# A decoder trunk's MLPs: where two plain blocks stand among the half products, and when one set of combinations is formed

## The chip, the cores and the metric

The kernel runs on one core of one Trainium2 chip. The metric is the device time of one execution in microseconds (us); several runs are taken and their median is compared. TensorE (PE) multiplies matrices, VectorE (DVE) and ScalarE (ACT) work on elements, GpSimd (POOL) and SyncE (SP) here mostly issue DMAs. PSUM is the small memory that PE writes to, in banks of 128 x 512 floats; everything else lies in SBUF.

## The reference

Two layers, 256 tokens, model width 2048, float32. Layer 0 mixes with gated linear attention, layer 1 with sliding-window attention; after each comes the MLP on which this case turns:

```
def sqrelu_mlp(h, w1, w2):
    u = jax.nn.relu(h @ w1)
    return (u * u) @ w2
# x += mixer(rmsnorm(x)); x += sqrelu_mlp(rmsnorm(x)); w1: 2048 x 8192, w2: 8192 x 2048
```

## The kernel before

**Numbers in two halves.** Every float32 product is made of three matmuls: a weight block `w` is split into `wh` (a rounded copy, a cast on ACT at L115) and `wl = w - wh` (a subtraction on DVE at L116), the activations likewise, and PE sums high x high, high x low and low x high. `halve` does a 512 x 512 block in two halves of 128 x 1024 each: two casts and two subtractions for a block. It has four `wh` tiles of half a block each (`WHL`), so a cast waits until PE has done with the half block four halves back; three `wl` tiles (`WS`) and three `ws` tiles, into which SP loads a block of 1 MB. The tiles of a pool are handed out in turn, so a load waits for the block three loads back.

**Seven products in the place of eight.** In most of the MLP, a pair of 512 x 512 output blocks is computed by Strassen's scheme (in Winograd's form) for two of the four row blocks of the weights, with the tokens cut into two halves: seven *half products* (12 matmuls of 128 x 512 each) of sums of weights and sums of activations take the place of eight, and two more row blocks come in as four *plain blocks* (24 matmuls each). A half product needs weights that are themselves sums. They are made in place: `wx` is loaded, then a DMA with addition (issued by POOL: L245 in W1, L1098 in W2) adds the next block to it once the earlier use is over; `wy` is added to a loaded block on DVE (L303, L1179), and a loaded block is added to `wx` on DVE (L321, L1194). A plain block costs ACT and DVE as much as a half product, and PE twice as much.

**Order of the work.** The MLP runs in four quarters of the 8192 hidden columns. In a quarter there are two pairs of columns of W1 (`two_columns`, with the class `Seven`), then two pairs of output columns of W2 (`seven`). In the first quarter the first pair is computed with `gemm_wide` instead, without sums; the combinations of the MLP's input that the half products of W1 need are formed there (`form_sums`, due `KEEP` ticks after the start; a tick comes twice for each plain or wide block, once for a half product), and written to DRAM to be fetched again in the later quarters. In W1 a string of steps sets the order: a digit n is half product `p`n, two digits "ij" are the plain block of row block i and column j, and "e" takes the sums E and F. The code of `seven` writes the order of W2 out: A0, plain 21, E2, plain 31, D4, C6, plain 20, plain 30, D5, A1, C3 (the letter is the bank, the number the operand). Below, half products of W2 are named that way, and those of W1 by their step.

**What orders the engines.** The Tile framework lays out each engine's instructions ahead of time, by priority and by its own estimate of when operands are there; casts, subtractions, loads and weight additions have a raised priority (`WPRI`). On the chip every engine then takes its instructions strictly in that order, and an instruction that waits holds up all behind it on its engine.

Of the kernel before, what the change touches and what calls it, by code (L numbers as in the profile page):

```python
# [21 lines left out]
C = 512  # L22
# [19 lines left out]
MX = 2  # L42
COMB = (1, 3)
ORDERS = "1 21 3 7 31 e 5 20 30 6 2 4", "21 1 31 3 7 e 5 20 30 6 2 4"
KEEP = 9, 11
SQ = (3, 2)
ATT = (5, 3), (9, 6), (10, 8), (11, 10)

# [2 lines left out]
def yoco_kernel(ctx: ExitStack, tc: tile.TileContext, x, norms, mlp_w1, mlp_w2, a_w_in, w_glr, w_gate, a_g_o, a_w_o,  # L51
# [12 lines left out]
    def bank(shape, tag, dtype=F32):  # L64
        return ps[tag].tile(shape, dtype, name=tag, tag=tag)
# [7 lines left out]
    def later(n, fn):  # L73
        due.setdefault(now[0] + n, []).append(fn)

    def tick():
        now[0] += 1
        for fn in due.pop(now[0], ()):
            fn()

    def mm(o, l, r, start=True, stop=True, **kw):
        nc.tensor.matmul(o, lhsT=l, rhs=r, start=start, stop=stop, **kw)  # L82
# [23 lines left out]
    def halve(ws, o=C, n=2):  # L106

        whs = [wp.tile([P, 2, C], F32R, name="wh", tag="wh", bufs=WHL) for _ in range(2)]
        wl = wp.tile([P, 4, C], F32R, name="wl", tag="wl", bufs=WS)
        with tc.high_priority(offset=WPRI):  # L110
            for k in range(0, 4, n):
                wh = whs[k // 2]
                js, ks = slice(k % 2, k % 2 + n), slice(k, k + n)
                w = ws[k // 2] if isinstance(ws, list) else ws[:, ks, :o]
                nc.scalar.copy(out=wh[:, js, :o], in_=w)  # L115
                nc.vector.tensor_sub(out=wl[:, ks, :o], in0=w, in1=wh.bitcast(F32)[:, js, :o])  # L116
        return [(whs[k // 2][:, k % 2], wl[:, k]) for k in range(4)]

    def split_w(parts, step=4):
        ws = wp.tile([P, 4, C], F32, name="ws", tag="ws", bufs=WS)  # L120
        with tc.high_priority(offset=WPRI):
            for k in range(0, 4, step):
                ks = slice(k, k + step)
                o = 0
                for ap in parts:
                    n = ap.shape[1]
                    nc.sync.dma_start(out=ws[:, ks, o:o + n],
                                      in_=ap[k * P:(k + step) * P].rearrange("(k p) n -> p k n", p=P))
                    o += n
        return halve(ws, o, min(step, 2))  # L130
# [85 lines left out]
    class Seven:  # L216
# [63 lines left out]

        def run(self, after, order="1 21 3 7 31 e 5 20 30 6 2 4"):

            for step in order.split():
                if len(step) == 2:
                    i, j = int(step[0]), int(step[1])
                    self.plain(i, j, *("EF" if j else "AC"))
                else:
                    (self.ef if step == "e" else getattr(self, "p" + step))(after)
# [28 lines left out]
        def p2(self, after):  # L317
            b21 = self.load(1, 0)
            with tc.high_priority(offset=WPRI):
                for n in range(2):  # L320
                    nc.vector.tensor_add(out=self.wx[n], in0=self.wx[n], in1=b21[:, 2 * n:2 * n + 2])  # L321
            self.product("A", self.token(1, 0), b21)
            after["a"](self.banks["A"])

        def p4(self, after):
            after["c"](self.product("C", self.token(1, 1), self.wx))
# [614 lines left out]
    def mlp(w1, w2, act, r, gains):  # L941
# [19 lines left out]
        def form_sums(pairs, es, b):  # L961

            combine_act(es, act, b, room)
            if b:
                for a, o in zip(pairs, kept):
                    nc.sync.dma_start(out=o, in_=a.bitcast(F32))
# [7 lines left out]
        def two_columns(col, es, hs, put):  # L974


            x = mp.tile([P, 4, C], F32, name="wx", tag="wx")
            add = lambda o, i, j: nc.vector.tensor_add(out=o, in0=i, in1=j)  # L978
            sub = lambda o, i, j: nc.vector.tensor_sub(out=o, in0=i, in1=j)  # L979
            h, ef = {}, []  # L980

            def relu(o, i, t):
                nc.scalar.activation(out=o, in_=i, func=AF.Relu, scale=r[:, t:t + 1])

            def turn(j, t, h):
                tp = bank([P, 4, P], "tp")
                for k in range(4):
                    nc.tensor.transpose(out=tp[:, k, :], in_=h[:, k * P:(k + 1) * P], identity=ident)  # L988
                put(j, slice(t * P, (t + 1) * P), tp)

            def p1(p):
                h["v"], h["22"] = hs()
                nc.scalar.mul(out=h["v"], in_=p, mul=-1.0)

            def p5(p):
                h["21"], h["12"] = hs()
                nc.scalar.copy(out=h["21"], in_=p)

            def p56(p):
                v, x21, x12, x22 = (h[i] for i in ("v", "21", "12", "22"))  # L1000
                add(v, p, v)
                add(x12, ef[0], v)
                relu(x12, x12, 0)
                later(1, lambda: turn(1, 0, x12))
                sub(x22, v, x22)
                add(x22, ef[1], x22)
                relu(x22, x22, 1)
                later(2, lambda: turn(1, 1, x22))
                sub(x21, x21, v)

            def p2(p):
                relu(h["v"], p, 0)
                later(1, lambda: turn(0, 0, h["v"]))

            def p4(p):
                add(h["21"], p, h["21"])
                relu(h["21"], h["21"], 1)
                later(1, lambda: turn(0, 1, h["21"]))

            z = Seven(lambda i, j: w1[i * C:(i + 1) * C, col[j]:col[j] + C], act, es,  # L1020
                      [x[:, 2 * i:2 * i + 2] for i in range(2)],
                      lambda: mp.tile([P, 4, C], F32, name="wy", tag="wy", bufs=1))
            z.run({"p1": p1, "p7": lambda p: nc.scalar.copy(out=h["22"], in_=p),
                   "ef": lambda e, f: ef.extend((e, f)), "p5": p5, "p56": p56, "a": p2, "c": p4}, ORDERS[1])

        def h_ops():
            n = iter(range(2))
# [16 lines left out]
        def pause(n):  # L1044

            pt = small()
            for i in range(n):
                mm(pt[:, i:i + 1], ident, ones[:, 0:1])
# [31 lines left out]
        def seven(w, n, op, us, g, acts, gains, sq, nr):  # L1080
# [6 lines left out]
            def block(i, j):  # L1087
                return w[i * C:(i + 1) * C, (c0 + j) * C:(c0 + j + 1) * C]
# [13 lines left out]
            def use(b):  # L1102
                if b in banks:
                    return banks[b], False
                banks[b] = bank([P, C], "ms" if b in "EF" else "acc")
                return banks[b], True

            def product(b, o, ws):
                p, st = use(b)
                halves = halve(ws)  # L1110
                for k in range(4):
                    wh, wl = halves[k]
                    mm(p, op[o][:, 0, k], wh, st and k == 0, False, skip_group_check=True)
                    mm(p, op[o][:, 0, k], wl, False, False, skip_group_check=True)
                    mm(p, op[o][:, 1, k], wh, False, k == 3, skip_group_check=True)
                tick()
                return p

            def plain(i, j, b0, b1, apart=False):

                halves = split_w([block(i, j)])
                ah, al, _ = us[i]
                ps_ = [use(b) for b in (b0, b1)]
                order = [(k, t) for k in range(4) for t in range(NT)]
                for n, (k, t) in enumerate(sorted(order, key=lambda kt: kt[1]) if apart else order):
                    wh, wl = halves[k]
                    p, st = ps_[t]
                    tt = slice(t * P, (t + 1) * P)
                    mm(p, ah[:, k, tt], wh, st and k == 0, False, skip_group_check=True)
                    mm(p, ah[:, k, tt], wl, False, False, skip_group_check=True)  # L1130
                    mm(p, al[:, k, tt], wh, False, k == 3, skip_group_check=True)
                    if n % 4 == 3:
                        tick()
# [47 lines left out]
            more(x, 1, 1)  # L1181
            add(x21, p)
            sub(x22, product("C", 6, y))
            for i in (2, 3):
                plain(i, 0, "A", "C", i == 2)
            add(v, product("D", 5, x))
            if g == 3:
                add(x12, v)
# [4 lines left out]
            with tc.high_priority(offset=WPRI):  # L1193
                nc.vector.tensor_add(out=x, in0=x, in1=b21)  # L1194
            product("A", 1, b21)
            add(x11, banks["A"])
            if g == n + 2 == 3 and not gains:

# [20 lines left out]
        for g in range(4):  # L1219
# [15 lines left out]
            else:  # L1235
                for b in range(2):
                    later(KEEP[b], lambda b=b, sums=sums, es=es: form_sums(sums, es, b))
                later(RS + 3, lambda: pause(2))
# [32 lines left out]
            for n in range(2):  # L1271
                seven(w, n, op, us, g, acts, gains, sq, nr)
# [241 lines left out]
```

## Time and profile before

| | |
|---|---|
| median of 3 runs | 2027.87 us (2027.11 to 2028.26) |
| the profiled execution | 2028.39 us, of which the span of its instructions is 2026.7 us |
| granted TensorE clock | 1.00 |
| busy | PE 2007.9 us (99%), DVE 1694.3 (84%), ACT 1307.3 (65%), POOL 236.7 (12%) |
| HBM | 461.23 MB read, 6.29 MB written |

A page's shares say which engine is busy, not which one waits: PE's matmuls overlap in the record (one of 128 x 512 is listed with 390 ns, while the next one starts 227 ns after it), so that PE looks busy also where its matmuls start late. The distance between starts shows it.

### The profile page before, as it was taken

What the parts mean: (1) busy time and instruction counts of PE and PEld (TensorE: products, weight loads), DVE (VectorE), ACT (ScalarE), POOL (GpSimd) and SP (SyncE); (2) the same over time, 40 slices, a digit from 0 to 9 for tenths busy, and PEclk for the clock granted to TensorE, in tenths of its full rate; (3) what the DMA queues carried; (4) which work ended last, traced back from release to release, by engine and by line L of the source; (5) the groups of instructions that cost most, each with busy time, mean ns of one, the idle gap of its engine ahead of it and who ended that gap; (6) DMA issues with size and microseconds to landing.
All of it is one profiled execution on the core that took longest, in us unless ns stands there. A gap on an engine that the chain in (4) does not pass through costs nothing.

```text
span 2026.7 us, 25842 instructions
## 1 busy us (share of the span) xinstructions
PE 2007.9 (99%) x9714; PEld 1660.9 (82%) x9714; DVE 1694.3 (84%) x1878; ACT 1307.3 (65%) x1724; POOL 236.7 (12%) x243
## 2 busy tenths in 40 slices
PE   9999999999999999999999999999999999999999
PEld 8998888887888788888788878788788888888887
DVE  6698787888888988987999676878988988988887
ACT  6746666666557657756767677656657756755765
POOL 2251110000010010001101121000010001101000
PEclk9999999999999999999999999999999999999999
DMA  8445775778898799888876543788799898889875
GB/s 287 146 156 177 216 220 188 204 248 253 264 294 251 229 297 263 231 281 267 237 225 193 166 137 122 206 261 248 225 301 262 231 282 272 237 259 294 256 228 147
DMA packets 237037, 469.21 MB, mean 232 GB/s; under 512 B 8704, under 2 KB 19216, under 8 KB 234864
## 3 DMA queue, kind: packets, MB, share of 16 engines
q1 hardware_dynamic: 195296, 380.92, 54.0%
q0 software_dynamic: 38528, 84.76, 22.5%
q10 hardware_dynamic: 3088, 1.88, 0.3%
q8 instruction: 76, 1.25, 0.2%
q14 instruction: 49, 0.40, 0.1%
HBM read 461.23 MB, written 6.29 MB: 231 GB/s over the span
## 4 chain that ended last, share of the span: by engine, by line
PE 70%; issue 10%; DVE 9%; DMA 8%; ACT 3%; POOL 1%; ACTq 0%; POOLq 0%; DVEq 0%
PE acc L82 51%; PE ms L82 14%; DMA wx<-in_mlp_w_dram 7%; DVE wl L116 5%; PE tp L82 3%; ACT sc L1397 1%; ACT wh L115 1%; DVE h L978 1%; PE tp L988 1%; DMA ws<-in_a_w_in_dram 1%; POOL wx L245 1%; PE tp L833 0%; DVE h L979 0%; DVE sc L1407 0%; DVE wx L321 0%
## 5 line engine op out<-in xcount | busy, mean ns | idle before, releaser
L82 PE MATMUL acc<-wh,act 128*128 128x512 f32 x2928 | 931.0, 392 | 1.2 <-ACT act L341 0.5
L115 ACT CAST wh<-ws 128x1024 fp32r<-128x1024 f32 x544 | 569.9, 1051 | 314.1 <-PE acc L82 235.4
L116 DVE TENSOR_TENSOR wl<-ws,wh 128x1024 fp32r<-128x1024 f32 x544 | 669.3, 1241 | 103.8 <-ACT wh L115 98.7
L82 PEld LDWEIGHTS acc<-wh,act 128*128 128x128 f32 x2928 | 548.3, 188 | 119.1 <-ACT wh L115 2.2
L82 PE MATMUL acc<-wl,act 128*128 128x512 f32 x1464 | 571.4, 390 | 1.2 <-DVE wl L116 1.2
L116 DVE TENSOR_TENSOR wl<-wx,wh 128x1024 fp32r<-128x1024 f32 x272 | 328.3, 1222 | 108.9 <-ACT wh L115 104.5
L115 ACT CAST wh<-wx 128x1024 fp32r<-128x1024 f32 x272 | 285.6, 1053 | 204.5 <-PE acc L82 100.9
L82 PEld LDWEIGHTS acc<-wl,act 128*128 128x128 f32 x1464 | 275.0, 188 | 58.0 <-DVE wl L116 2.1
L82 PE MATMUL ms<-wh,act 128*128 128x512 f32 x512 | 166.7, 393 | 2.1 <-DVE act L1268 2.1
L82 PE MATMUL acc<-act,wh 128*128 128x256 f32 (+1 forms) x640 | 141.4, 308 | 0.9 <-ACT wh L403 0.9
L115 ACT CAST wh<-wy 128x1024 fp32r<-128x1024 f32 x92 | 96.1, 1054 | 62.3 <-PE ms L82 49.9
L116 DVE TENSOR_TENSOR wl<-wy,wh 128x1024 fp32r<-128x1024 f32 x92 | 111.1, 1222 | 20.8 <-ACT wh L115 19.0
L82 PE MATMUL acc<-wh,ops 128*128 128x512 f32 (+1 forms) x392 | 124.8, 390 | 0.6 <-DVE h L978 0.6
L245 POOL DMA_DIRECT2D wx<-in_mlp_w_dram x56 | 67.9, 1237 | 485.1 <-DVE wl L116 424.1
L82 PE MATMUL acc<-wh,op 128*128 128x512 f32 x384 | 123.4, 389 | 0.0
L82 PEld LDWEIGHTS ms<-wh,act 128*128 128x128 f32 x512 | 95.5, 188 | 25.6 <-DVE act L1268 5.5
L1098 POOL DMA_DIRECT2D wx<-in_mlp_w_dram x32 | 41.2, 1287 | 597.4 <-DVE wl L116 583.0
L82 PEld LDWEIGHTS acc<-act,wh 128*128 128x128 f32 x640 | 104.5, 191 | 6.6 <-ACT wh L403 1.1
L82 PE MATMUL acc<-act,wl 128*128 128x256 f32 x384 | 107.9, 283 | 0.6 <-DVE wl L404 0.6
L82 PE MATMUL ms<-wl,act 128*128 128x512 f32 x256 | 99.8, 390 | 0.0
L82 PE MATMUL tp<-wh,cmb 128*128 128x512 f32 x288 | 94.5, 389 | 0.0
L82 PEld LDWEIGHTS acc<-wh,ops 128*128 128x128 f32 x392 | 72.6, 188 | 15.3 <-ACT wh L115 1.6
(298 smaller groups left out, 2571.6 us busy)
## 6 DMA issues: line engine op xcount, KB each, us to landing
ws<-in_mlp_w_dram SPq DMA_DIRECT2D x196, 1024.0 KB, 7.0
ws<-in_a_w_in_dram SPq DMA_DIRECT2D x42, 1024.0 KB, 5.1
wx<-in_mlp_w_dram POOLq DMA_DIRECT2D x32, 1024.0 KB, 9.1
wy<-in_mlp_w_dram SPq DMA_DIRECT2D x30, 1024.0 KB, 7.4
wx<-in_mlp_w_dram POOLq DMA_DIRECT2D x56, 512.0 KB, 8.6
wx<-in_mlp_w_dram SPq DMA_DIRECT2D x16, 1024.0 KB, 5.0
ws<-in_b_w_q_dram SPq DMA_DIRECT2D x16, 1024.0 KB, 5.1
ws<-in_a_w_o_dram SPq DMA_DIRECT2D x15, 1024.0 KB, 5.2
```

Source lines behind the costliest of these rows:

```text
L82: nc.tensor.matmul(o, lhsT=l, rhs=r, start=start, stop=stop, **kw)
L115: nc.scalar.copy(out=wh[:, js, :o], in_=w)
L116: nc.vector.tensor_sub(out=wl[:, ks, :o], in0=w, in1=wh.bitcast(F32)[:, js, :o])
L245: nc.gpsimd.dma_start(out=o, in_=a, accum_op=ALU.add)
L978: add = lambda o, i, j: nc.vector.tensor_add(out=o, in0=i, in1=j)
L988: nc.tensor.transpose(out=tp[:, k, :], in_=h[:, k * P:(k + 1) * P], identity=ident)
L1098: nc.gpsimd.dma_start(out=ws, in_=block(i, j).rearrange("(k p) n -> p k n", p=P), accum_op=ALU.add)
L1397: nc.scalar.activation(out=sc[:, h], in_=sc[:, h], func=AF.Exp, bias=nmx[:, h:h + 1], scale=f[:, h:h + 1], accum_out=su[:, h:h + 1])
```

## The change

1. In W1 (`two_columns`) the order "21 1 31 3 7 e 5 20 30 6 2 4" becomes "1 21 3 31 5 7 20 e 6 2 30 a 4". The new step "a" hands bank A on after plain block 30 and not after `p2`, since 30 still adds to A.
2. In W2 (`seven`) plain block 30 moves from its place behind plain 20 to a place behind A1: D4, C6, plain 20, D5, A1, plain 30, C3.
3. `KEEP` goes from 9, 11 to 5, 7: the combinations of the MLP's input are formed four ticks sooner in the first quarter.

No matmul, cast, addition or byte is added or taken away.

```
-KEEP = 9, 11
+KEEP = 5, 7
...
         def run(self, after, order="1 21 3 7 31 e 5 20 30 6 2 4"):
+            self.late = "a" in order
             for step in order.split():
-                if len(step) == 2:
+                if step == "a":
+                    after["a"](self.banks["A"])
+                elif len(step) == 2:
...
             self.product("A", self.token(1, 0), b21)
-            after["a"](self.banks["A"])
+            if not self.late:
+                after["a"](self.banks["A"])
...
-                   "ef": lambda e, f: ef.extend((e, f)), "p5": p5, "p56": p56, "a": p2, "c": p4}, ORDERS[1])
+                   "ef": lambda e, f: ef.extend((e, f)), "p5": p5, "p56": p56, "a": p2, "c": p4}, "1 21 3 31 5 7 20 e 6 2 30 a 4")
...
-            for i in (2, 3):
-                plain(i, 0, "A", "C", i == 2)
+            plain(2, 0, "A", "C", True)
             add(v, product("D", 5, x))
...
             product("A", 1, b21)
+            plain(3, 0, "A", "C")
             add(x11, banks["A"])
```

The first place to see in the layout is DVE in W2, around D5 and A1, in the second pair of the third quarter. `wx` holds D5's weights, the block under L1194 (now L1197) is b21, A1's weight block; the `wl` behind it are A1's. Before:

```order
L116 TENSOR_TENSOR wl_7576<-ws_7572,wh_7574 128x1024
L1136 TENSOR_TENSOR xs_3309<-xs_3309,acc_7518 128x512
L116 TENSOR_TENSOR wl_7576<-ws_7572,wh_7575 128x1024
L116 TENSOR_TENSOR wl_7607<-wx_7378,wh_7605 128x1024
L116 TENSOR_TENSOR wl_7607<-wx_7378,wh_7606 128x1024
L1194 TENSOR_TENSOR wx_7378<-wx_7378,ws_7625 128x2048
L116 TENSOR_TENSOR wl_7630<-ws_7625,wh_7628 128x1024
L116 TENSOR_TENSOR wl_7630<-ws_7625,wh_7629 128x1024
```

And now:

```order
L116 TENSOR_TENSOR wl_7543<-ws_7539,wh_7542 128x1024
L116 TENSOR_TENSOR wl_7574<-wx_7378,wh_7572 128x1024
L1140 TENSOR_TENSOR xs_3309<-xs_3309,acc_7518 128x512
L116 TENSOR_TENSOR wl_7574<-wx_7378,wh_7573 128x1024
L1197 TENSOR_TENSOR wx_7378<-wx_7378,ws_7592 128x2048
L116 TENSOR_TENSOR wl_7597<-ws_7592,wh_7595 128x1024
L116 TENSOR_TENSOR wl_7597<-ws_7592,wh_7596 128x1024
L116 TENSOR_TENSOR wl_7618<-ws_7614,wh_7616 128x1024
```

D5's two subtractions, the addition and A1's two now come directly behind plain 20 (wl_7543), and those of plain 30 (wl_7576 before, wl_7618 now) behind them.

The second place is DVE a little later, where W2 ends and the next quarter's W1 begins. ws under L303 (now L306) is b12, the block to which `wy` is added for p7. Before, with C3's halves (wl_7650), plain 21's (wl_7684), p1's (wl_7720) and plain 31's (wl_7745):

```order
L116 TENSOR_TENSOR wl_7650<-wx_7378,wh_7649 128x1024
L116 TENSOR_TENSOR wl_7684<-ws_7680,wh_7682 128x1024
L1135 TENSOR_TENSOR xs_3267<-acc_7380,xs_3267 128x512
L116 TENSOR_TENSOR wl_7684<-ws_7680,wh_7683 128x1024
L116 TENSOR_TENSOR wl_7720<-wx_7679,wh_7718 128x1024
L116 TENSOR_TENSOR wl_7720<-wx_7679,wh_7719 128x1024
L1135 TENSOR_TENSOR xs_3267<-acc_7518,xs_3267 128x512
L303 TENSOR_TENSOR ws_7795<-ws_7795,wy_7774 128x2048
L116 TENSOR_TENSOR wl_7745<-ws_7741,wh_7743 128x1024
```

And now, with the second half of plain 30 (wl_7618), C3 (wl_7650), p1 (wl_7685) and plain 21 (wl_7710):

```order
L116 TENSOR_TENSOR wl_7618<-ws_7614,wh_7617 128x1024
L116 TENSOR_TENSOR wl_7650<-wx_7378,wh_7648 128x1024
L116 TENSOR_TENSOR wl_7650<-wx_7378,wh_7649 128x1024
L116 TENSOR_TENSOR wl_7685<-wx_7679,wh_7683 128x1024
L1139 TENSOR_TENSOR xs_3267<-acc_7380,xs_3267 128x512
L306 TENSOR_TENSOR ws_7819<-ws_7819,wy_7741 128x2048
L116 TENSOR_TENSOR wl_7685<-wx_7679,wh_7684 128x1024
L116 TENSOR_TENSOR wl_7710<-ws_7706,wh_7708 128x1024
```

The addition to b12 now stands in the middle of p1's subtractions, ahead of plain 21's, with four instructions between it and the subtraction that frees the tile b12 is loaded into: that of plain 30 (wl_7618). Before, b12's tile was that of A1's block, and nine instructions stood between. The layout is alike at the start of W1 in each quarter but the first.

## The prediction

> **What bounds the kernel now.** I read the page's busy times first, then the matmuls' spacing in the timeline and the chain of waits, then who waits for PE and for whom PE waits, and last the DMA queues.
>
> ```profile
> span 2026.7 us, 25842 instructions
> PE 2007.9 (99%) x9714; PEld 1660.9 (82%) x9714; DVE 1694.3 (84%) x1878; ACT 1307.3 (65%) x1724; POOL 236.7 (12%) x243
> 855.16 27.20 PE acc L82 x120
> 850.00:900.00 50.00, 50.00 (x222) 41.42 (x221) 43.26 (x42) 28.26 (x27) 3.85 (x3) 1.00 0.88 264
> 950.00:1000.00 50.00, 49.65 (x224) 40.09 (x223) 45.89 (x48) 36.82 (x45) 4.86 (x4) 1.00 0.79 234
> ```
>
> The third row is a piece of the chain of waits: 120 matmuls in 27.20 us, 0.2267 us apart, is PE's own pace; long stretches of the MLP run at it. The last two rows are 50 us of the third and fourth quarter: DVE works 43 to 46 of the 50 us, and the DMA engines are 0.79 to 0.88 busy. So PE sets the time, the change takes no matmul away, and it can win only what PE now loses by starting late. Those losses stand in few places:
>
> ```profile
> 467.64 0.39 PE L82 MATMUL acc<-wh,cmb 128*128 128x512 f32 x1
> 468.90 0.50 PE L82 MATMUL acc<-wl,cmb 128*128 128x512 f32 x1 [0.87 <-DVE wl L116]
> 490.94 0.39 PE L82 MATMUL acc<-wh,act 128*128 128x512 f32 x1
> 491.80 0.50 PE L82 MATMUL acc<-wl,act 128*128 128x512 f32 x1 [0.47 <-DVE wl L116]
> 960.90 0.39 PE L82 MATMUL acc<-wh,act 128*128 128x512 f32 x1
> 961.49 0.47 PE L82 MATMUL acc<-wh,act 128*128 128x512 f32 x1 [0.20 <-DVE h L978]
> 1009.56 0.40 PE L82 MATMUL ms<-wl,act 128*128 128x512 f32 x1
> 1010.15 0.73 PE L82 MATMUL ms<-wh,act 128*128 128x512 f32 x2 [0.20 <-DVE act L1268]
> PE ms L82 <- DVE act L1268: 2.1, 8, 0.3
> ```
>
> Starts 1.26, 0.86, 0.59 and 0.59 us apart where 0.23 would do: (i) p3 of the first quarter, late by 1.03; (ii) the end of W1 in the first quarter; (iii) the step from W1's first pair to its second; (iv) the step from W1 to W2, where plain 21 waits for activations that only the last half products give (the last row: in each of the eight quarters). Everywhere else in the MLP the matmuls keep their pace, which means that `wh` and `wl` are there in time, not that they are early.
>
> **The change, part by part.** *What it can win.* Adding up the same spacings over 0.2267 in each place: (iii) 0.3 to 1.1 us in six quarters, mean 0.6, so 3.8; (iv) 0.7 to 1.6, mean 0.8, so 4.9 in six quarters, of which I take 4, since p6's results now come 36 matmuls (8.2 us) ahead of W1's end and not 24; (ii) 2.3 in each layer's first quarter, of which I take 1.75, 3.5; (i) 1.5 with its neighbours in each layer, of which I take 1, so 2, because the two combination stores now stand ahead of three loads on SP. If forming the combinations sooner delays the first quarter's own operands, it costs as much as it gives: (i) from -3 to +3. Sum of the gains 13.3 (0 to 18).
>
> *W2: D5 and A1 come sooner, their operand doesn't.* In 16 places D5 now starts 48 matmuls after D4, 10.88 us, where it was 72, 16.32. D5's weights are `wx` plus a block that POOL may only add once DVE is done with D4:
>
> ```profile
> 893.47 1.28 POOL L1098 DMA_DIRECT2D wx<-in_mlp_w_dram  x1 [12.05 <-DVE wl L116]
> 895.80 0.39 PE L82 MATMUL acc<-wh,op 128*128 128x512 f32 x1
> 853.28 1.28 POOL L1098 DMA_DIRECT2D wx<-in_mlp_w_dram  x1 [15.39 <-DVE wl L116]
> 855.00 0.39 PE L82 MATMUL acc<-wh,op 128*128 128x512 f32 x1
> DMA to landing us min/median/max: 8.4/9.1/12.7
> wx<-in_mlp_w_dram POOLq DMA_DIRECT2D x1, 1024.0 KB, 11.4
> wx<-in_mlp_w_dram POOLq DMA_DIRECT2D x1, 1024.0 KB, 10.9
> ```
>
> The issue is 2.3 us ahead of D4's first matmul in the second pair (2.2 over its eight places) and 1.7 in the first. The fifth row is the source line of all 32 such DMAs; the last two are the first and last of the second pairs' eight, whose mean is 10.1 us (the first pairs' eight: 9.2). So the sum lands 7.9 us after D4's start in the second pair and 7.4 in the first. What DVE then has to do in its order is read from the order shown with the change and from these rows:
>
> ```profile
> 900.19 2.35 DVE L116 TENSOR_TENSOR wl<-ws,wh 128x1024 fp32r<-128x1024 f32 x2
> 902.46 0.68 DVE L1136 TENSOR_TENSOR xs<-xs,acc 128x512 f32<-128x512 f32 x1
> 903.06 1.22 DVE L116 TENSOR_TENSOR wl<-ws,wh 128x1024 fp32r<-128x1024 f32 x1
> 909.23 2.29 DVE L1194 TENSOR_TENSOR wx<-wx,ws 128x2048 f32<-128x2048 f32 x1
> 911.44 1.22 DVE L116 TENSOR_TENSOR wl<-ws,wh 128x1024 fp32r<-128x1024 f32 x1
> L115 ACT CAST wh<-wx 128x1024 fp32r<-128x1024 f32 x272 | 285.6, 1053 | 204.5 <-PE acc L82 100.9
> ```
>
> Start to start a subtraction takes 1.13 us, a 512-wide addition 0.60, the addition of b21 2.21; the last row is the cast, 1.05. From the landing: cast 1.15 with its waits, subtraction 1.13, addition to xs 0.60, subtraction 1.13, b21 2.21, A1's first subtraction 1.22: 7.45 us. A1 begins 60 matmuls after D4 and needs that half at its second matmul, at 13.6 + 0.23 = 13.83. So A1 is late by whatever the landing exceeds 6.4 us after D4's start. Second pairs: 7.9 - 6.4 = 1.5 each, 12 in eight. First pairs: 7.4 - 6.4 = 1.0; but the waits of (iv) go, and with them two additions of L1268 (0.69 each) from DVE's work ahead of D4, so that the issue comes about 0.7 sooner: 0.3 each, 2 in eight. Together 14 us; bounds 2, if all land in the 8.4 us of the quickest with that 0.7, and 27, if the second pairs take 12 us and the first keep their 1.0. Before, the same DMA had 5.4 us more, and PE never waited here.
>
> *W1: the addition for p7 stands in p1's way.* In six places (the first pair of W1 in the later quarters) DVE reaches b12's addition (L303) with only the loads' own time behind it. SP can load b12 once plain 30's second subtraction is done. From the landing of D5's weights that is: 7.45 - 1.22 to the start of A1's first subtraction, then 1.13, 1.13, 1.13 and 0.60 to that of plain 30's second half, and its 1.22: 11.4. The load has its rows before, the quickest and slowest of these six:
>
> ```profile
> ws<-in_mlp_w_dram SPq DMA_DIRECT2D x1, 1024.0 KB, 5.8
> ws<-in_mlp_w_dram SPq DMA_DIRECT2D x1, 1024.0 KB, 8.1
> 923.43 2.28 DVE L303 TENSOR_TENSOR ws<-ws,wy 128x2048 f32<-128x2048 f32 x1
> DVE wl L116 <- ACT wh L115: 222.2, 233, 4.6
> ```
>
> Mean 7.2. Then the addition, 2.2, and p1's second subtraction, 1.22: at 22.1. PE needs that half in p1's eighth matmul: A1 starts at 7.2 on the same clock, A1, plain 30 and C3 are 48 matmuls, 10.9, and 1.6 more: 19.7. Late by 2.4 each, 1.0 to 3.3 with the two rows: 14 us in six (6 to 20). DVE's long waits now are for ACT's casts (last row), short ones for loads. The second pair has the same addition in the same place, but there DVE has five more additions ahead of it and reaches it when the block is just there: 0 to 0.5 each. Behind the addition wait plain 21's and p3's subtractions on DVE; plain 21 gives them 5.4 us of PE for 2.3 of DVE, so nothing else is late.
>
> *p5 to p6.* 48 matmuls from p5's start to p6's, not 60 (10.9 us, not 13.6), and `wx` must be summed again between:
>
> ```profile
> 938.05 1.20 POOL L245 DMA_DIRECT2D wx<-in_mlp_w_dram  x1 [12.94 <-DVE wl L116]
> 939.42 1.20 POOL L245 DMA_DIRECT2D wx<-in_mlp_w_dram  x1 [0.17 <-issue]
> 939.32 0.39 PE L82 MATMUL tp<-wh,cmb 128*128 128x512 f32 x1
> ACT wh L115 <- DMA wx<-in_mlp_w_dram: 67.9, 30, 4.2
> DMA to landing us min/median/max: 5.9/8.4/12.0
> ```
>
> ACT waits here already (67.9 us in 30 waits). The second issue came 0.1 us after p5's start; with the median 8.4, a cast and a subtraction the half is there at 10.9, and p6 needs it at 10.9 + 1.6 = 12.5. p5 now stands behind a plain block, which gives its casts 2.7 us more lead: I take 0 to 1 us in all 14 pairs together, 1; with landings of 12 it is 2 each, 28.
>
> By the Trainium skill, "DMA: Bandwidth & Descriptors", section "Anatomy of one DMA — SWDGE (gpsimd) path", a DMA of POOL's kind takes about 2.0 us plus its bytes over 436e3 per us, an estimate of 4.4 us for the 1 MB of D5. By that A1 would never be late and the W2 term were 0. The 32 rows here, 8.4 us at the least, don't agree; it is the first rival's price in W2, no more.
>
> *Sum.* 14 + 14 + 1 + 1 - 13.3 = +16.7, with 1 for b12's addition in the second pairs; I take +16. The profiled execution is 2028.4 us, 0.5 above the median of the runs and inside their range: 2044.
>
> **The rivals.** *Only the gains* (faster): D5's sum and b12 land sooner than before, because the new order spreads the loads, and PE keeps its pace; 2028.4 - 13 = 2015. For it: DVE's and PE's work is unchanged, and losses (i) to (iv) are real. Against: none of the 32 additions landed in under 8.4 us, at DMA shares of 0.8 to 0.9. Chance 0.15. *Gains and losses cancel*: landings at their short ends, W2 2 to 4 and b12 6, against 10 to 13 gained; 2028. It needs both at once. 0.15. *p6 decides* (slower still): the second addition into `wx` lands after 10 us or more, so that each of 14 p6 is late by 1 to 2; it begins to cost at 10.0 us after p5's start, and adds some 21 to the forecast, 2065. For it: ACT's 30 waits; against it: the longer lead of p5. 0.12. The forecast itself 0.58.
>
> **How the numbers follow.** The likeliest is 2044, its own range 2032 to 2056 from the bounds of the two large terms, which will not all be met at one end. To hold 8 in 10 the range takes in "cancel" and stops short of most of the other two: 2022 to 2060. A difference of 0.2% (4 us) is what runs of this kernel tell from none. Faster: the first rival and a little of the second, 0.15. Same: the rest of the second and the forecast's low end, 0.15. Slower: 0.70.
>
> **What would show it.** W2: DVE's idle time ahead of D5's subtractions ended by a late cast, ACT's cast of `wx` ended by the DMA of line 1098's kind in all 16 places, and A1's second matmul 0.5 to 2 us late. W1: DVE idle ahead of the addition to b12, ended by the load of `ws`, and p1's eighth matmul late by 1 to 3 us in six places, not in the second pairs. (iii) and (iv) gone. If DVE doesn't wait at b12's addition, or A1 keeps PE's pace, the terms fall and the first rival is right; if p6 stands out, the third.

## The result and the profile after

The changed kernel takes 2086.4 us (median of four runs, 2083.1 to 2087.7), the kernel before 2027.5 beside it: 1.029 times as long (95% interval 1.027 to 1.031). The forecast was slower, 2044 us, with 2060 as the upper end of its range: the direction was right, the loss 3.7 times as large as forecast (59 us, not 16). The profiled execution of the changed kernel took 2083.1 us. The head of its page, which answers the first two rows shown of before:

```profile
span 2081.4 us, 25838 instructions
PE 2020.6 (97%) x9714; PEld 1668.6 (80%) x9714; DVE 1700.1 (82%) x1878; ACT 1311.9 (63%) x1724; POOL 238.2 (11%) x243
```

The span is 54.7 us longer and DVE has no more work than before (1700 us, 1694 before). PE's 2020.6 says little, since waiting matmuls are listed as busy in part; the list of waits says more. Of the changed kernel, for whom an engine waited, with the sum in us, the number of waits and the longest:

```profile
PE acc L82 <- DVE wl L116: 21.5, 6, 4.7
PE acc L82 <- DVE xs L1140: 16.1, 16, 2.9
PE acc L82 <- ACT h L1027: 12.1, 11, 2.7
DVE ws L306 <- DMA ws<-in_mlp_w_dram: 22.0, 6, 5.3
```

The first and the last belong together: six waits of PE behind b12's addition, as forecast but longer. The second and third are new, and neither waits for weights. L1140 in its 16 places takes C6 from `xs`, L1027 copies p7: both only *read a PSUM bank*, and PE waits because it wants to write there next.

Added up over the matmuls of each step, distance from start to start less PE's own pace (0.2267 us for 128x512, 0.07 allowed for a transpose), over 14 pairs of W1 and 15 of W2 (the last pair of W2 has another form):

| us over the pace | before | after |
|---|---|---|
| p1 of W1 | 0.5 | 27.7 |
| plain 20 of W1 | 0.0 | 15.8 |
| plain 20 of W2 | 0.4 | 21.7 |
| plain 30 and p4 of W1 | 1.8 | 7.6 |
| plain 21 of W1 | 8.2 | 7.4 |
| A0, plain 21, E2 of W2 | 14.9 | 4.2 |
| p3 and p2 of W1 | 5.2 | 0.0 |
| D5 and A1 of W2 | 0.0 | 0.1 |
| all steps | 30.7 | 85.1 |

The difference, 54.4 us, is nearly all of the longer span. Each transpose comes some 0.04 us later than the 0.07 allowed, so that the rows with transposes (plain 21, 30 and p4 of W1, A0 to E2 of W2) hold some of these too, and not only waits. D5 and A1, where the forecast put its first 14 us, lose nothing.

**Plain 20 of W2.** The timeline of the place that the prediction's order shows (third quarter, second pair; POOL, ACT, DVE, then PE):

```profile
910.75 1.28 POOL L1102 DMA_DIRECT2D wx<-in_mlp_w_dram  x1 [12.59 <-DVE wl L116]
919.41 2.00 ACT L115 CAST wh<-wx 128x1024 fp32r<-128x1024 f32 x2 [2.32 <-DMA wx<-in_mlp_w_dram]
920.49 1.23 DVE L116 TENSOR_TENSOR wl<-wx,wh 128x1024 fp32r<-128x1024 f32 x1 [1.77 <-ACT wh L115]
921.63 0.68 DVE L1140 TENSOR_TENSOR xs<-xs,acc 128x512 f32<-128x512 f32 x1
922.23 1.22 DVE L116 TENSOR_TENSOR wl<-wx,wh 128x1024 fp32r<-128x1024 f32 x1
921.04 0.39 PE L82 MATMUL acc<-wh,act 128*128 128x512 f32 x1
922.37 0.50 PE L82 MATMUL acc<-wh,act 128*128 128x512 f32 x1 [0.94 <-DVE xs L1140]
```

D5's sum lands at 919.3, ACT casts it, DVE subtracts the first half at 920.49, and only then comes L1140, which could have run at 918.7. Plain 20 does one token half into bank A and then, from its 13th matmul on, the other into bank C, which L1140 still reads: PE stands from 921.3 to 922.4. D5's and A1's halves, which come after, are then in time. Before, the same read was done at 903.14 (the prediction's row of L1136: 902.46 and 0.68), 0.8 us before PE wrote there: plain 20 began at 901.2, and its 13th matmul stood at 903.9.

**Plain 20 of W1.** Third quarter, first pair; L1027 is the copy of p7's bank C. ACT, then PE:

```profile
785.59 0.57 ACT L1001 COPY h<-tp 128x512 f32<-128x512 f32 x1
786.27 1.06 ACT L115 CAST wh<-wx 128x1024 fp32r<-128x1024 f32 x1
789.09 1.04 ACT L115 CAST wh<-wx 128x1024 fp32r<-128x1024 f32 x1 [1.76 <-DMA wx<-in_mlp_w_dram]
790.04 0.58 ACT L1027 COPY h<-acc 128x512 f32<-128x512 f32 x1
788.74 0.39 PE L82 MATMUL acc<-wl,act 128*128 128x512 f32 x1
790.67 0.50 PE L82 MATMUL acc<-wh,act 128*128 128x512 f32 x1 [1.55 <-ACT h L1027]
```

It is the same pattern on another engine: ACT's cast for p6 waits for its DMA, the copy is behind it, and plain 20, which adds to bank C, may not write there yet. p6 itself is never late.

**p1 of W1.** Fourth quarter, first pair; POOL, DVE, PE:

```profile
931.13 0.55 POOL L976 DMA_DIRECT2D cmb<-kept  x1 [4.87 <-PE acc L82]
940.59 2.29 DVE L306 TENSOR_TENSOR ws<-ws,wy 128x2048 f32<-128x2048 f32 x1 [4.10 <-DMA ws<-in_mlp_w_dram]
942.80 1.22 DVE L116 TENSOR_TENSOR wl<-wx,wh 128x1024 fp32r<-128x1024 f32 x1
944.08 0.80 PE L82 MATMUL acc<-wl,act 128*128 128x512 f32 x1 [3.50 <-DVE wl L116]
```

The addition waits for b12's load, p1's second subtraction for the addition, PE for that. The load was issued at 930.9 and landed at 940.5; 0.2 us behind it the second of the stored sets of combinations was fetched.

**A slower TensorE behind the long stops.** Stretches around that stop, with the busy time of PE, PEld, DVE, ACT and POOL, the granted clock, DMA share and GB/s:

```profile
938.00:942.00 4.00, 2.57 (x12) 1.80 (x10) 1.41 (x1) 2.82 (x3) 0.00 (x0) 1.00 1.02 333
944.00:946.50 2.50, 2.42 (x6) 1.95 (x7) 2.50 (x4) 0.00 (x0) 1.21 (x1) 0.50 0.24 29
946.50:950.00 3.50, 3.50 (x15) 2.80 (x14) 2.75 (x3) 1.79 (x3) 0.00 (x0) 0.89 0.95 175
```

For 2.5 us after the stop the clock is 0.50 and matmuls come 0.427 us apart. Six such runs, 48 matmuls, cost 9.6 us, which are in the table's rows. So the 54.7 us are made of 22.5 of waits at p1, some 20 and 16 at the two plain blocks 20 and 9.6 of slow matmuls, 68 together, less what the other rows of the table gained.

### The profile page after: what moved, and what is told of

The parts are those of the page before. It is cut to its first block, busy times and chain, and to the rows that moved or that the text cites. A ratio compares the mean times of both kernels' runs of the same rounds, so it can differ in the third digit from the quotient of the medians.

```text
span 2081.4 us, 25838 instructions
## 1 busy us (share of the span) xinstructions
PE 2020.6 (97%) x9714; PEld 1668.6 (80%) x9714; DVE 1700.1 (82%) x1878; ACT 1311.9 (63%) x1724; POOL 238.2 (11%) x243
## 4 chain that ended last, share of the span: by engine, by line
PE 56%; DMA 19%; issue 13%; DVE 7%; ACT 4%; POOL 1%; ACTq 0%; POOLq 0%; DVEq 0%; SPq 0%
PE acc L82 44%; DMA wx<-in_mlp_w_dram 17%; PE ms L82 6%; PE tp L82 4%; DVE wl L116 3%; ACT wh L115 2%; DMA ws<-in_mlp_w_dram 1%; ACT sc L1401 1%; DMA ws<-in_a_w_in_dram 1%; PE tp L992 1%; DVE xs L1140 1%; PE tp L837 1%; POOL wx L245 0%; DVE sc L1411 0%; PE tp L1333 0%
## 5 line engine op out<-in xcount | busy, mean ns | idle before, releaser
L82 PE MATMUL acc<-wh,act 128*128 128x512 f32 x2928 | 954.4, 397 | 28.2 <-DVE xs L1140 16.1
L116 DVE TENSOR_TENSOR wl<-wy,wh 128x1024 fp32r<-128x1024 f32 x92 | 111.1, 1221 | 27.6 <-ACT wh L115 27.5
L82 PEld LDWEIGHTS ms<-wh,act 128*128 128x128 f32 x512 | 95.5, 188 | 19.4
L82 PE MATMUL acc<-wh,cmb 128*128 128x512 f32 x264 | 87.2, 392 | 0.0
```

## The experiments

In the diffs, - and + are against the kernel named. Times stand beside runs of the kernel before in the same session (2026.2 in the first four, 2026.8 in the next four, 2026.1 in the last).

**The three parts alone** (against the kernel before). W2:

```
-            for i in (2, 3):
-                plain(i, 0, "A", "C", i == 2)
+            plain(2, 0, "A", "C", True)
...
             product("A", 1, b21)
+            plain(3, 0, "A", "C")
```

> The kernel before with the change in W2 alone (plain block 30 behind A1); W1's order and KEEP as before. Two theories of W2's loss. Bank theory, formed from the trace of the change: D5's weights are late, and DVE, which waits for their first half, has the subtraction of C6 from xs (the read of bank C) behind it in its order; PE wants to write plain 20's second token half into that bank and waits 0.7 to 3 us in each of the 16 places, at plain 20's 13th matmul, while D5 and A1 keep PE's pace. Then 16 x 1.3 = 21 us are lost and nothing else: 2027.5 + 21 = 2048 us (2044 to 2053). Recorded theory: the loss is at A1's second matmul, 14 us in 16 places, 2041 us, and plain 20 keeps its pace. If neither place is late, W2's part costs nothing alone: 2027.

Measured: 2073.9 us, ratio 1.024 (1.023 to 1.026), 47.7 slower. Its waits:

```profile
PE acc L82 <- DVE xs L1136: 25.1, 16, 3.6
PE acc L82 <- DVE wl L116: 14.8, 10, 2.6
DVE ws L303 <- DMA ws<-in_mlp_w_dram: 22.6, 7, 4.6
```

The place is the bank theory's, A1 loses nothing, but the size is not: plain 20 loses 34 us (slow matmuls included), since D5's sum lands 6.85 us after D4's start here and 6.2 in the whole change. And there is a second loss that I had put down to W1: b12's addition stands between the subtractions of the plain block that opens W1, 14 us more than before. It comes with W2's move, because b12's load waits for plain 30.

The order of W1 (with the code for the step "a"):

```
-  ..., "a": p2, "c": p4}, ORDERS[1])
+  ..., "a": p2, "c": p4}, "1 21 3 31 5 7 20 e 6 2 30 a 4")
```

> The kernel before with the new order of W1 alone; W2 and KEEP as before. By the trace of the change, W1 loses in three places: p1's 8th matmul behind b12's addition (22.5 us in six places), the first matmul of plain 20 into bank C behind ACT's copy of that bank, which stands behind p6's casts (15.8 us in 14 places), and some 10 us of matmuls at 0.43 us start to start after the long stalls; it gains some 13 us in the steps from W1's first pair to its second and from W1 to W2. If W1's losses are its own: about 2027.5 + 35 = 2063 us (2055 to 2070), with the p1 stalls at 4 to 5 us each, since b12's load waits for A1's second subtraction here, which comes later before p1 than plain 30's does in the change. If they come only together with W2's change (b12's load waits for plain 30, which W2 now puts last): p1 is not late, and the time is 2027 to 2035 us. The recorded sizes give 2033.

Measured: 2045.1 us, ratio 1.009 (1.007 to 1.011), 18.9 slower. p1 is nowhere late (0.8 us in 14 places); plain 20 loses 32.9 us:

```profile
PE acc L82 <- ACT h L1027: 24.0, 13, 3.1
```

Neither expectation holds as a whole: p1's stops need both parts, the bank's stops belong to W1's order alone.

KEEP:

```
-KEEP = 9, 11
+KEEP = 5, 7
```

> The kernel before with KEEP = 5, 7 alone. The trace of the change shows p3 of the first quarter no longer late in either layer (3.4 us before). If forming the combinations sooner costs the first quarter nothing: 2027.5 - 3 = 2024.5 us (2023 to 2026). If the sooner stores and casts hold up the wide blocks by as much: 2027.5 (2026.5 to 2029).

Measured: 2018.0 us, ratio 0.9961 (0.9946 to 0.9975): 8.2 us *faster*, with KEEP = 3, 5 below the best kernel of this study. p3, p2 and p4 of the first quarter lose 0.1 us where they lost 6.2 in both layers together. The three parts alone add up to 47.7 + 18.9 - 8.2 = 58.4 us, the whole change costs 58.9; that the sum fits is partly luck, since the places differ.

**C6's read ahead of D5's subtraction** (against the change). One pair of DVE's instructions changes places in each pair of W2, nothing else on any engine:

```
-            sub(x22, product("C", 6, y))
+            read = sub(x22, product("C", 6, y))
...
-            add(v, product("D", 5, x))
+            with tc.issue_after(read.ins):
+                p = product("D", 5, x)
+            add(v, p)
```

> The change, with one pair of DVE's instructions exchanged in each place of W2: the subtraction of C6 from xs (the read of bank C) stands ahead of D5's first subtraction and not behind it. D5's operand is as late as in the change. Bank theory: plain 20's wait at its 13th matmul goes in all 16 places, and A1, which had some 1.4 us to spare while PE stood still for 1.1, keeps its pace or is late by under 0.3: 2086.4 - 21 = 2065 us (2061 to 2069). Operand theory (the recorded one: the sum for D5 and A1 is late whatever stands between): the wait moves to A1's second matmul, 0.7 to 1.5 us in each of 16 places, and the time stays at 2077 to 2086 us.

Measured: 2065.0 us, ratio 1.019 (1.018 to 1.021), 21 us less than the change. Its DVE timeline at the same place (L1140 now first):

```profile
913.09 0.69 DVE L1140 TENSOR_TENSOR xs<-xs,acc 128x512 f32<-128x512 f32 x1
914.69 2.36 DVE L116 TENSOR_TENSOR wl<-wx,wh 128x1024 fp32r<-128x1024 f32 x2 [0.92 <-ACT wh L115]
```

D5's sum comes as late as in the change (6.24 us after D4's start, 6.23 there); plain 20 loses 0.2 us in 15 places, D5 and A1 together 2.2, of which 1.8 in the one pair whose DMA took 11.1 us. The bank theory is shown; the recorded one falls. Plain 20 of W1 loses 22.9 us here, 7 more than in the change, and p1 some 4 less; neither was followed up.

**p7's copy ahead of p6's casts** (against the change):

```
-            after["p7"](self.product("C", self.op(3), b12))
+            self.copied = after["p7"](self.product("C", self.op(3), b12))
...
-            after["p56"](self.product("D", self.op(1), self.wx))
+            with ExitStack() as order:
+                if self.late:
+                    order.enter_context(tc.issue_after(self.copied.ins))
+                p = self.product("D", self.op(1), self.wx)
+            after["p56"](p)
```

> The change, with ACT's copy of p7's bank C (L1027) ahead of p6's two casts in the MLP's W1; all else follows from the layout. p6's weights are as late as in the change. Bank theory (the copy held behind a cast that waits for its DMA is what stops plain 20 in W1): the 15.8 us that plain 20 of W1 loses in 14 places go, p6 keeps its pace since its second half has some 2.9 us to spare: 2086.4 - 16 = 2070 us (2066 to 2075). Operand theory: p6's 8th matmul takes the wait over, 0.5 to 2 us in most of the 14 places: 2080 to 2088.

Measured: 2073.1 us, ratio 1.023 (1.020 to 1.025). Plain 20 of W1 falls from 15.8 to 0.9 us and p6 keeps its pace, as the bank theory has it. The profiled execution, one of the longer ones, took 2077.2 us; in it p1 and plain 20 of W2 lose 3 us each more than in the change's profile, and plain 30 and p4 some 3 more together. The layout also moved other instructions of DVE, ACT and PE here, so this experiment is less clean than the one before.

**b12's addition later** (against the change):

```
             b12 = self.load(0, 1)
-            with tc.high_priority(offset=WPRI):
+            with ExitStack() as order:
+                order.enter_context(tc.high_priority(offset=WPRI))
+                if self.late:
+                    order.enter_context(tc.issue_after(self.sub.ins))
                 nc.vector.tensor_add(out=b12, in0=b12, in1=self.y)
```

`self.sub` is plain 31's last subtraction.

> The change, with b12's addition (the one for p7) put behind plain 31's second subtraction on DVE in W1, where it stood between p1's two. Its load is as late as before. If p1 waits only because that addition stands in its way: the 27.7 us at p1 and some 5 us of slow matmuls behind it in plain 21 go: 2086.4 - 32 = 2054 us (2048 to 2060). If p1's own operand is as late (the same loads behind the same plain 30): p1 still waits, 1 to 3 us each, and the time is 2068 to 2082.

Measured: 2124.7 us, ratio 1.048 (1.045 to 1.050), far off. p1's loss does go, 27.7 to 0.8 us, but plain 20 of W1 now loses 89. The lines of this kernel stand a little lower (L117 the cast, L1033 the copy); its waits:

```profile
ACT wh L117 <- DMA wx<-in_mlp_w_dram: 108.6, 39, 5.1
PE acc L82 <- ACT h L1033: 60.8, 14, 6.3
```

and its timeline at the place of W1 that the change's rows showed at 789, ACT and PE:

```profile
796.45 1.04 ACT L117 CAST wh<-wx 128x1024 fp32r<-128x1024 f32 x1 [3.11 <-DMA wx<-in_mlp_w_dram]
797.40 0.58 ACT L1033 COPY h<-acc 128x512 f32<-128x512 f32 x1
798.03 0.79 PE L82 MATMUL acc<-wh,act 128*128 128x512 f32 x1 [5.80 <-ACT h L1033]
```

The addition (2.3 us) now stands ahead of p5's subtractions on DVE. These release POOL's two DMAs into `wx`. At this place they are issued 4.0 and 2.6 us ahead of p5's start in the change, 2.0 and 0.9 here, and they land after 9.4 and 12.4 us, not 8.4 and 9.9; the cast waits for them, the copy for the cast, PE for the copy. The stop moved from p1 to the bank and grew.

**All three together** (against the change: the three diffs above).

> The change, with all three: C6's read first, p7's copy first, b12's addition later. Bank theory with the addition in the way: each loss has its own cause, so 2086.4 - 21 - 16 - 32 = 2017 us (2010 to 2025), faster than the kernel before. If the three waits cover for one another (each stop gave the next operand time): 2030 to 2055.

Measured: 2052.6 us, ratio 1.013 (1.011 to 1.014). Both plain blocks 20 and p1 are clean (0.9 us, under 0.3 and 0.8); now p6 (6.2 us), p2 (19.4) and plain 30 (12.6) are late. ACT's waits for the DMAs into `wx`, of the change and of this kernel:

```profile
ACT wh L115 <- DMA wx<-in_mlp_w_dram: 48.3, 26, 4.3
ACT wh L117 <- DMA wx<-in_mlp_w_dram: 79.1, 38, 3.3
```

The time is in the rival's range, but that the change's own stops had covered for one another is not shown. p6 is late because the sum in `wx` is, and p2's subtractions stand behind p6's on DVE. That sum lands 10.0 us after p5's start, mean of 14, as in the change with the addition's move alone (10.2); the change itself has 6.5, and the kernel of the next experiment, with the copy first and W2 as before, 7.3. So the third fix makes the sum late itself; with the copy first, plain 20 no longer hides it. A kernel with the first two fixes alone was not run. No stop in its MLPs is followed by slow matmuls.

**W1's order, KEEP and the copy first, W2 as before** (the order and KEEP of the change, and the copy's diff, on the kernel before).

> The kernel before with the new order of W1, KEEP = 5, 7, and p7's copy ahead of p6's casts; W2 as before. With W1's order alone plain 20 lost 32.9 us in 14 places and the whole was 18.9 slower than before, so that the rest of the order gains 14; KEEP alone gained 8.2. Bank theory: 2026.2 - 14 - 8 = 2004 us (2000 to 2011). If the wait moves to p6: 2015 to 2035.

Measured: 2019.8 us, ratio 0.9969 (0.9959 to 0.9978): 7 us faster than before, where KEEP alone gained 8.2. Plain 20 is clean (1.4 us) and p6 keeps its pace. The order's gain at its joints is not there.

**Without the second fetch** (against the change). The combinations that p3 and p7 use in the later quarters are set to zero by POOL; 1 MB less is loaded at the start of each:

```
-                    nc.gpsimd.dma_start(out=a.bitcast(F32), in_=o)
+                    if o is kept[1]:
+                        nc.gpsimd.memset(a.bitcast(F32), 0.0)
+                    else:
+                        nc.gpsimd.dma_start(out=a.bitcast(F32), in_=o)
```

> The change, with the second set of stored combinations set to zero by POOL in the later quarters and not fetched (1 MB less at each quarter's start; the values that p3 and p7 multiply there are left out, all instructions on the other engines stay). In the change b12's load takes 8.4 to 10.8 us in the six places where p1 waits, mean 9.6, and the fetch is issued 0.2 us behind it. Contention theory: without the fetch the load takes the 7.2 us that the prediction took from before, p1's stalls shrink from 3.7 to some 1.3 us each and the slow matmuls behind them go: 2086.4 - 14 - 7 = 2065 us (2059 to 2071). Rival (the two loads of wx behind it, or HBM alone, make it slow): the load stays above 9 us and the time at 2080 to 2088.

Measured: 2064.0 us, ratio 1.018 (1.017 to 1.020). The order on DVE, ACT, PE and SP is the change's to the instruction. b12's load, of the change the quickest and the slowest of the six (KB, us from issue to landing):

```profile
ws<-in_mlp_w_dram SPq DMA_DIRECT2D x1, 1024.0 KB, 8.4
ws<-in_mlp_w_dram SPq DMA_DIRECT2D x1, 1024.0 KB, 10.8
```

and without the fetch, two of its six (7.2 to 7.7, mean 7.5):

```profile
ws<-in_mlp_w_dram SPq DMA_DIRECT2D x1, 1024.0 KB, 7.4
ws<-in_mlp_w_dram SPq DMA_DIRECT2D x1, 1024.0 KB, 7.7
```

DVE's waits for it there, 22.0 us in the change:

```profile
DVE ws L306 <- DMA ws<-in_mlp_w_dram: 10.1, 5, 2.2
```

p1 loses 11.4 us where it lost 27.7, 1.7 in each of the six, and no slow run follows it; plain 20 of W1 loses 21.6, 5.8 more than in the change. The fetch beside the load is what made it 9.6 us long on average.

**KEEP = 3, 5** (against the kernel before).

> The kernel before with KEEP = 3, 5. With 5, 7 alone the time was 2018.0 and the first quarter's W1 loses nothing any more (p3, p2 and p4: 7 us before in both layers, 0.3 then). If the combinations only have to be there in time, two ticks more give nothing: 2018 us (2016.5 to 2019.5). If sooner is better for the loads too: 2013 to 2016. If the stores now collide with the wide blocks' loads: 2020 to 2027.

Measured: 2018.5 us, ratio 0.9959 (0.9943 to 0.9975), the same as with 5, 7. In time is enough.

**W1's order with the copy first, alone** (against the kernel before).

> The kernel before with W1's new order and p7's copy ahead of p6's casts; W2 and KEEP as before. It tells whether W1's order has a gain of its own. If the order gains at its joints (first to second pair, W1 to W2) as the prediction has it, apart from KEEP's gain: with KEEP the time was 2019.8, so 2019.8 + 8.2 = 2028 would mean that it gains nothing at all; if the joints' 7.8 us are real and KEEP's gain is the same as what the order gives in the first quarter: 2018 to 2021. My reading of the trace is between: the order and KEEP take away the same late starts in the first quarter (p3, p2, p4), and the joints give under 2.5 us: 2022 us (2020 to 2025).

Measured: 2022.0 us, ratio 0.998 (0.997 to 0.999), as the trace's reading had it: what the order gains, 4 us, lies in the first quarter, where KEEP gains it too.

**W2's change alone, with C6's read first** (against the kernel before: the W2 diff and the read's diff).

> The kernel before with W2's change alone and C6's read of bank C ahead of D5's first subtraction. W2's change alone cost 47.7 us, of which the trace puts 34 at plain 20's second token half, 5 in slow matmuls and 14 more than before at the plain block that opens W1 (b12's addition stands between its subtractions and waits for a load that waits for plain 30). Bank theory: the 34 and most of the 5 go and the 14 stay: 2026.5 + 14 + 2 = 2042 us (2037 to 2047). Operand theory: A1 takes the wait over, 2055 us or more. If the read first frees the rest too: 2027 to 2032.

Measured: 2053.5 us, ratio 1.013 (1.010 to 1.016), between the two theories. Plain 20's 34 us are gone, but D5, A1 and plain 30 now lose 9.2 (the sum lands 6.9 us after D4's start here), and the plain block that opens W1 loses 27.6 where it lost 22.1, slow matmuls included. Without W1's order the sum is later than A1 can bear. Why b12's stop grew by 5 us was not followed up.

## Why the prediction was right and wrong

**Direction.** Right. In W2 D5's operand has 5.4 us less, and b12's load comes when W1 begins: both cost time, as forecast, but in W2 not by the wait that was forecast. (The base of 2028.4 is 0.1 us above the runs' range and not inside it, which changes nothing.)

**"W2: A1 is late by whatever the landing exceeds 6.4 us": the step that failed.** The sum landed 6.23 us after D4's start, mean of 15 (the DMA took 8.7 us, 10.1 and 9.2 forecast, and was issued 0.5 us sooner). But A1 kept its pace also where it landed late: at 8.16 us in the change and at 8.04 and 8.88 with W2's change alone, where the rule asks for a lateness of 1.6 to 2.5, A1 lost nothing and plain 20 lost 3.2, 3.1 and 5.5.

What was missed is what stands *between*: the prediction quotes the 0.68 us read of bank C and counts it as 0.60 in DVE's chain, and never asks who waits for it. From the rows it had, the working is short. The read ends 3.0 us after the landing (cast, one subtraction, itself). PE writes that bank 36 matmuls after D4's start, 8.16 us. Late by landing + 3.0 - 8.16, the landing less 5.2. So PE stops there before A1's limit is met, and A1, put back by the same stop, has time left. The forecast's own 7.4 and 7.9 give 2.2 and 2.7 in each place, 39 us (34 with the 0.7 that it took off in the first pairs); the measured 6.23 gives 1.1, and 21 were lost with the few long ones. A1's lateness shows only with the read first: 0.33, 0.50 and 1.79 us at landings of 6.96, 7.10 and 8.43, a limit of 6.6, where the prediction's terms without the read give 7.0. The 14 us of the forecast came out near the 21 by luck.

**"W1: the addition for p7 stands in p1's way": right in place and cause, too small.** Six places, none in the second pairs, DVE idle ahead of the addition, p1's eighth matmul late: all as forecast. Its term was 2.4 us each, 14; measured 3.75, 22.5. The failing term is the load's 7.2 us, taken from the kernel before, where the same fetch was issued 2.1 us ahead of the load and landed some 3 us into it. In the change the load took 9.6 with the fetch 0.2 us behind it, and 7.2 to 7.7 when the fetch was left out. The lateness grew by less than the load, since plain 20's stop puts A1 back too: it starts 8.6 us after the landing in all six places, not 7.2. The start of the load was right: 11.4 us after the landing (930.7 by the rule, 930.9 in the trace).

**"p5 to p6: 0 to 1 us in all, 1": wrong.** p6 keeps its pace, as said. But ACT's wait for `wx`, which the prediction names with 67.9 us in 30 waits, has p7's copy behind it, and plain 20 waits for that copy: 15.8 us, 32.9 with W1's order alone. The third rival, p6 late by 1 to 2, names the same sum, but that landed 6.5 us after p5's start, soon enough for p6; what it held up was the copy.

**The gains, 13.3.** (i) and (ii), 5.5 forecast: p3, p2 and p4 of the first quarter, 6.2 us, did go; KEEP alone brings 8.2. The prediction gave 2 of it to KEEP and 3.5 to W1's order; the order with the copy first brings 4.1 alone and adds nothing to KEEP. (iii) and (iv), 7.8 forecast: nothing beyond KEEP's gain (7.0 with the order and the copy first, 8.2 without). In the change's own table the joints' rows fall by 11.5 us, but plain 30 and p4, where the transposes now stand, take back 5.8, and they lose some 12.5 once plain 20 is clean (the two runs with W1's order, the copy first and W2 as before). The list of waits of before gave only 2.1 us for L1268. Much of what the prediction read as late starts at the joints is the transposes' own spacing, which moves with the order: in the change four of them at 850.1 take 0.2 us more than the table allows, with no wait. The list of waits was the safer measure there. (p6's results come 48 matmuls ahead of W1's end now, not the 36 counted.)

**No term for a slower clock.** 9.6 us came from matmuls after long stops.

**The rule quoted from the Trainium skill** ("DMA: Bandwidth & Descriptors", "Anatomy of one DMA — SWDGE (gpsimd) path"; 4.4 us, an estimate by its figures for 1 MB of POOL's kind) is not borne out by the change either: its 32 DMAs took 8.4 to 10.8 us, mean 9.0.

## What to carry to other kernels

For each instruction that an operand makes late, list what stands behind it on its engine, and ask of every *read of a PSUM bank* in that list which matmul writes the bank next: the reader is short, the stop is not. Price a moved load with the transfers that will run beside it in its new place. And when an instruction is moved out of one operand's way, look for what it now stands ahead of, before adding the gains: b12's addition, moved behind plain 31, made the sum for p6 some 3.5 us later.

## What was not expected of the hardware

After a stop of PE, matmuls of 128x512 come 0.427 us apart, at a granted clock of 0.50, for 5 to 13 matmuls, most often 7 or 8. Over the MLPs of the kernel before, the change and the twelve experiments, counted by the time by which one start came late: none of 16 stops of 1.5 to 1.75 us was followed by such a run, 18 of 46 between 1.75 and 3.25, 7 of 10 between 3.25 and 3.75, and all 18 above. Each slow matmul costs 0.2 us, so that a stop of 4 us costs 5 to 6.6.

The Trainium skill, "TensorE: Matmul & The Clock Gate", Part 1, "The HAM clock gate", says that the clock falls to half after an idle window of about 3.4 us and is released after a busy one, and that the windows run freely. Eight matmuls at 0.427 us are 3.4 us, which agrees, though runs of 5 and of 13 occur; and free-running windows would make the outcome of a stop depend on where it falls, as seen. That a stop of under 2 us can be enough (1.93 with W2's change alone) doesn't follow from an idle window of 3.4; the measurement decides.

The second finding is how a fetch of 1 MB, issued 0.2 us behind a load of 1 MB, lengthened that load from 7.5 to 9.6 us on average: the later transfer delayed the earlier one. Issued 2.1 us ahead, as in the kernel before, it did not: the load took 7.2, though there no other load of SP was still under way.
